# A feature-major prologue with pipelined modulation, and a new order of the S5 tables in a hybrid S5, attention and experts layer

## The chip, the cores and the metric

One core of a Trainium2 chip. The metric is the device time of one launch in microseconds (us); less is better. An execution of this kernel repeats within about 0.3%.

## What is computed

One layer over 512 latent tokens `x` and 256 context tokens `ctx`, 1024 features, all in float32. Only the latent stream leaves the layer. Cut to what matters here:

```python
mod_x = silu(c) @ w_ada + b_ada            # 6 x 1024; mod_c from c_ctx in the same way
hx = rmsnorm(x, g1) * (1 + sc1x) + sh1x    # hc from ctx in the same way
u, qa, kva, kr, gates = split(hx @ w_in)   # 512 | 384 | 256 | 32 | 2048 columns; for hc without the gates
attn = mla(qa, [kv_c, kv_x], [kr_c, kr_x]) @ w_mla_o          # 8 heads, latents see context and latents
lam_bar, b_bar = discretise(lam, log_dt, b)                   # complex, 32 groups x 64 states, 2 directions
y = d * u + sum over directions of Re(c_out @ scan(lam_bar, b_bar @ u))   # state starts from the context's
ssm = (gelu(y) * sigmoid(gelu(y) @ w_glu + b_glu)) @ w_ssm_o
x = x + g1x * ((sigmoid(g_ssm) * ssm + sigmoid(g_attn) * attn) @ w_out)
x = x + g2x * expert_choice(modulated rmsnorm(x))             # 16 SwiGLU experts of width 2816, 64 tokens each
```

## The kernel before

Float32 weights and activations are split into two float32r parts (`hi`, `lo`), and a product is three matmuls (`mm3`, L121 to L124: L122 hi*hi, L123 hi*lo, L124 lo*hi). All up to L983 is one stage whose order on each engine is as written (`tc.manual_schedule()`, L212); the attention, the merge and the experts behind it are ordered by the framework. `dma` issues on SyncE's queue. T, V, S, G in the code are TensorE (PE), VectorE (DVE), ScalarE (ACT) and GpSimd (POOL).

**Prologue.** X (32 context and 64 latent rows of eight tokens each) is loaded token-major in eight DMAs, then `craw`, `braw` and the 16 tiles of the first third of `w_ada`. ACT squares X with a row sum, `xnorm` (L332) makes the reciprocal root mean square and VectorE scales X; `xt_half` (L344) turns X into feature-major tiles `xTa`, `xTb` (latent) and `hc` (context) with 64 PE transposes and their evictions. Between these, VectorE works out the S5 tables (exponentials, powers `lp`, their spreads `lt` and `lq` at L409, rotations `e8`, `bbar` from `bbar_g` at L454). `ada_part` (L189) makes the modulation with 32 output rows for each of four column blocks; `ada_end` (L193) copies it (`adar`), turns it into columns by eight small transposes (`adac`) and adds the bias (`acol`), from which `ab` follows. Then a loop over eight blocks of 128 features (L634 to L644) makes `hi` on ACT, `hxf` and `lo` on VectorE.

**Projection.** `w_in` is taken in 25 blocks of 128 columns (four `u`, two `kv`, three `q`, sixteen `g` for gates) and `kr`. `win_prep` (L609) splits a loaded block (`raw` pool) into `ws` (ACT copy, VectorE subtraction). `win_block` (L651) is 24 matmuls `px`, three for each feature block; `ctx_block` (L659) is 8 x 2 matmuls `pc` for the context. `fill_one` draws the next block after the `u` blocks in the order of L600, as work for PE between the steps of the S5 branch.

**S5 branch**, four groups `gb` of channels. `s5_P` (L508; ten operations on GpSimd, tile `PT`), `s5_Q` (L522; ten on VectorE), `s5_R` (L572; a table of powers by doubling, 24 multiplies and adds on GpSimd, tile `R`), `s5_B` (transposes `pbt` of Q), `s5_K` (L548; matmuls `pkc` of PT, copies `kc` on VectorE, DMAs that lay out `M`), `s5_V` (L756; matmuls `pv`, twelve products `za`, `zb` and sums, two scans at L778, eight operations to `Xc`), `s5_Y` (L790; `py` from M and U, L801 `py` from PT and Xc), `s5_T` and `s5_out`. `PT`, `R` and `ptmp` have two buffers each. Group order: P(0) and R(0) are issued in the prologue, Q(0) ahead of u0, B(0) behind u1, K(0), P(1), R(1) behind u2; in the loop (L842) stand V, two blocks, Q of the next group, Y, U of the next, P and R of the group after the next, a block, T, a block, then K and B of the next group.

**Behind it** attention and merge, with the other two thirds of `w_ada` (`wada_tiles`, L1173, 1 MB a DMA), then the experts, whose weights (2 MB a DMA) go through a ring of ten buffers in the memory that the attention part leaves.

## Time and profile before

| | |
|---|---|
| runs | 1924.98, 1919.36, 1923.01 us, median 1923.01 |
| profiled execution | 1919.85 us, its span 1918.1 us |
| granted TensorE clock, mean | 0.965 |
| PE, busy | 1633.8 us (85%) |
| DVE, busy | 531.5 us (28%) |
| ACT, busy | 320.7 us (17%) |
| POOL, busy | 209.9 us (11%) |
| read from HBM | 623.93 MB |

The experts take from about 650 us to the end; the change lies in the first 270 us. A row of a timeline gives start, duration, engine, line, operation, output and inputs with their shapes, and in brackets the idle time ahead of it and what ended that. A windows row gives busy time and number of instructions for each engine, the granted clock as a share of 2.4 GHz, the DMA share and GB/s.

### The profile page before, as it was taken

The numbers are of one execution on the slowest core, as the hardware profiler recorded it, in microseconds if no ns is written. First come the engines' busy times: TensorE is split into PE (matmuls) and PEld (weight loads), VectorE is DVE, ScalarE is ACT, GpSimd is POOL, SyncE is SP. The second block draws the span as 40 slices with busy tenths as digits, with TensorE's granted clock in tenths as the row PEclk, the third lists the DMA queues.
The fourth block names the chain that finished last, engine by engine and source line by source line (L and its number), as shares of the span: only waits on it lengthen the run. The fifth ranks groups of instructions, "written<-read, shape, count | busy, mean of one in ns | idle before, by whom it ended". The sixth has DMA issues, their size and how long they took to land.

```text
span 1918.1 us, 20921 instructions
## 1 busy us (share of the span) xinstructions
PE 1633.8 (85%) x8660; PEld 791.5 (41%) x8660; DVE 531.5 (28%) x1180; ACT 320.7 (17%) x593; POOL 209.9 (11%) x218
## 2 busy tenths in 40 slices
...
GB/s 316 57 141 111 105 189 133 170 97 201 157 90 401 363 422 426 422 427 420 422 427 422 421 426 422 426 423 423 425 421 427 421 427 421 420 428 421 427 422 281
DMA packets 108654, 642.56 MB, mean 335 GB/s; under 512 B 10256, under 2 KB 45072, under 8 KB 73232
## 3 DMA queue, kind: packets, MB, share of 16 engines
...
q14 instruction: 26, 0.21, 0.0%
HBM read 623.93 MB, written 17.27 MB: 334 GB/s over the span
## 4 chain that ended last, share of the span: by engine, by line
PE 43%; DMA 36%; DVE 8%; issue 5%; ACT 3%; POOL 2%; POOLq 0%; ACTq 0%; SPq 0%; DVEq 0%
DMA wgu<-in_w_e_gu 18%; PE pgu L1505 14%; DMA wd<-in_w_e_down 10%; PE pdn L1520 8%; DMA wd<-in_w_e_down_end 6%; PE pxg L1462 2%; PE po L1263 1%; DVE hd L94 1%; PE px L122 1%; PE px L124 1%; PE px L123 1%; ACT hd L1507 1%; PE ada L191 1%; PE phT L1512 1%; PE py L801 1%
## 5 line engine op out<-in xcount | busy, mean ns | idle before, releaser
L1505 PE MATMUL pgu<-wgu,xe 128*64 128x512 f32 (+1 forms) x3072 | 644.9, 559 | 27.5 <-DMA wgu<-in_w_e_gu 26.0
L1505 PEld LDWEIGHTS pgu<-wgu,xe 128*64 128x64 f32 x3072 | 219.9, 137 | 426.5 <-issue 351.1
L1520 PE MATMUL pdn<-wd,hT 128*64 128x512 f32 x1408 | 357.5, 645 | 34.5 <-ACT hT L1514 34.5
L94 DVE TENSOR_TENSOR hd<-hd,pgu 64x512 f32<-64x512 f32 x96 | 61.9, 645 | 994.3 <-ACT hd L1507 994.3
L1507 ACT ACTIVATE hd<-pgu 64x512 f32<-64x512 f32 x96 | 53.3, 556 | 951.5 <-PE pgu L1505 951.5
L1520 PEld LDWEIGHTS pdn<-wd,hT 128*64 128x64 f32 x1408 | 110.9, 146 | 214.2 <-issue 163.6
L1539 POOL DMA_INDIRECT out<-ye,sidx x16 | 24.9, 1556 | 1340.7 <-DVE ye L112 1340.7
L1512 PE MATMUL phT<-pk,hd 64*128 64x64 f32 x352 | 42.1, 236 | 126.7 <-DVE hd L94 126.7
L1512 PEld LDWEIGHTS phT<-pk,hd 64*128 64x128 f32 x352 | 29.0, 138 | 204.3 <-DVE hd L94 204.3
L122 PE MATMUL px<-hx,ws 128*128 128x512 f32 x200 | 81.1, 406 | 6.3 <-ACT hx L637 6.3
L123 PE MATMUL px<-hx,ws 128*128 128x512 f32 x200 | 80.1, 400 | 3.5 <-DVE hx L94 3.4
L124 PE MATMUL px<-hx,ws 128*128 128x512 f32 x200 | 79.5, 398 | 1.4 <-DVE ws L94 1.4
L1462 PE MATMUL pxg<-xm,oh 128*64 128x512 f32 x256 | 75.3, 609 | 0.6 <-DVE oh L94 0.6
L1514 ACT COPY hT<-phT 128x256 f32<-128x256 f32 x96 | 34.1, 355 | 119.2 <-PE phT L1512 119.2
L122 PEld LDWEIGHTS px<-hx,ws 128*128 128x128 f32 x200 | 38.4, 192 | 15.3 <-ACT hx L637 6.4
L123 PEld LDWEIGHTS px<-hx,ws 128*128 128x128 f32 x200 | 38.1, 190 | 14.7 <-DVE hx L94 7.6
L124 PEld LDWEIGHTS px<-hx,ws 128*128 128x128 f32 x200 | 38.2, 191 | 10.2 <-DVE ws L94 2.5
L1466 DVE COPY xg<-pxg 128x256 f32<-128x256 f32 x16 | 6.8, 424 | 127.1 <-ACT xg L1465 127.1
L1462 PEld LDWEIGHTS pxg<-xm,oh 128*64 128x64 f32 x256 | 30.6, 140 | 21.1 <-issue 19.4
L1233 DVE TENSOR_REDUCE mx<-ps 128x1 f32<-128x768 f32 x32 | 30.5, 954 | 27.7 <-PE ps L124 25.0
L354 PE MATMUL xT<-pk,X 96*128 96x96 f32 x64 | 11.5, 348 | 29.1 <-DMA craw<-in_ssm_c 18.7
L191 PE MATMUL ada<-wada,scv 128*32 128x512 f32 x192 | 34.1, 675 | 0.0
...
## 6 DMA issues: line engine op xcount, KB each, us to landing
wgu<-in_w_e_gu SPq DMA_DIRECT2D x176, 2048.0 KB, 37.9
...
```

Source lines behind the costliest of these rows:

```text
L94: (e or V).tensor_tensor(o, a, b, op=op)
L122: T.matmul(o, a[0], b[0], start=first, stop=False)
L123: T.matmul(o, a[0], b[1], start=False, stop=False)
L124: T.matmul(o, a[1], b[0], start=False, stop=last)
L191: T.matmul(p[32 * q:32 * q + 32, :], scv[:, k].rearrange("p s n -> p (s n)"), w[q], start=(k == 0), stop=(k == 7))
L1233: V.tensor_reduce(mx, p[:, 0:768], AX.X, ALU.max, negate=True)
L1462: T.matmul(px[64 * h:64 * h + 64, :], oh[:, t], xms[t][:, 512 * h:512 * h + 512], start=(t == 0), stop=(t == 3))
L1505: T.matmul(p[64 * j:64 * j + 64, :fn], xe[:, k, :], wt_[8 * j + k], start=(k == 0), stop=(k == 7))
L1507: S.activation(hd[:, :fn], p[0:64, :fn], AF.Silu)
L1512: T.transpose(ph[:, b, :], hd[:, 128 * b:128 * b + 128], ident[0:64, 0:64])
L1514: S.copy(hT[:, :n], ph[:, :n])
L1520: T.matmul(po[64 * h:64 * h + 64, :], hT[:, b, :], w[:, 512 * h:512 * h + 512], start=(f0 == 0 and b == 0), stop=(f0 + 128 * b == FF - 128))
```

## The change

- The host lays out `x` and `ctx` feature-major (`xt`, `ct`) and `w_in`, `w_kr` and `w_ada` by blocks, so that a partition's part of a tile is one run of 2 to 4 KB. The loads write 128 partitions each. The order on SyncE's queue is now: parameters, four `xt` and two `ct` pieces, six `w_ada` tiles of 1 MB, u0, four `w_ada` tiles of 512 KB, u1 to u3, `braw`, `craw`, `wkr`.
- The transposes, their evictions and the scaling of X go. `sums` squares on ACT (12 operations) and adds on VectorE (15 operations in `acc`), six matmuls sum over the features, `rstd` is [128, 6], and six matmuls spread it over the partitions in PSUM (`rb`).
- `lp`'s later powers, the two spreads and `bbar_g` are functions of their own: `powers_lp` and the spread of `lq` stand behind the `ada` matmuls, `bbar_g`, Q(0) and the spread of `lt` behind the first two `u` blocks.
- The modulation loop makes `hxf` one step ahead on VectorE (with `rb`), `hi` on ACT, `lo` on VectorE, and PE does the six matmuls of u0 and u1 for that feature block within the loop, into `px01`.
- P(0) is issued behind Q(0) and `lt`; R(0) on VectorE, R(1) on GpSimd. In the loop K(gb) stands first; P(gb+1) stands behind Y(gb) in place of P(gb+2), and `PT` has one buffer. One gate block more is drawn ahead of the loop. `uf` has two buffers. The three copies of `f_kr` go to ACT. The later `w_ada` tiles come in two DMAs of 512 KB each. The tail has four steps in place of five.

```diff
-                 ("rt", 1), ("rr", 2), ("xc", 1), ("pt", 2), ("m4", 2), ("uu", 1), ("yb", 1)):
+                 ("rt", 1), ("rr", 2), ("xc", 1), ("pt", 1), ("m4", 2), ("uu", 1), ("yb", 1),
+                 ("uf", 2)):
...
-    xv = A["x"].rearrange("(c l) d -> c l d", l=L)
-    cv = A["ctx"].rearrange("(c l) d -> c l d", l=L)
-    X = []
-    for j in range(4):
-        t = tl("xx", f"X{j}", [NCH, 2, D])
-        dma(t[0:NCX], cv[:, 2 * j:2 * j + 2, :])
-        dma(t[NCX:NCH], xv[:, 2 * j:2 * j + 2, :])
-        X.append(t)
+    hc = tl("hxp", "hc", [128, 8, 256])
+    xt = [tl("pt", "xTa", [128, 4, 512]), tl("bt", "xTb", [128, 4, 512])]
+    for i in range(2):
+        for j in range(2):
+            k = 2 * j
+            dma(xt[i][:, k:k + 2, :], A["xt"][i, :, k:k + 2, :])
+        dma(hc[:, 4 * i:4 * i + 4, :], A["ct"][:, 4 * i:4 * i + 4, :])
+    wt = {}
+    def wada_load(kh, tags):
...
+    wada_load(0, ["hxp", "hxp"])
+    wada_load(1, ["hxp", "hxp"])
+    wada_load(2, ["ws", "ws"])
+    order = [(f, b) for f, bs in (("u", range(4)), ("g", (0, 1, 2)), ("kv", (0,)), ("g", (3, 4, 5)), ("kv", (1,)),
+                                  ("g", (6, 7, 8)), ("q", (0, 1)), ("g", (9, 10)), ("q", (2,)), ("g", range(11, 16)))
+             for b in bs]
+    base = {"u": 0, "q": 4, "kv": 7, "g": 9}
+    wins, preps = [], {}
+    nxt = {"load": 0, "prep": 0}
...
+    win_load()
+    wada_load(3, ["m4", "m4", "zz", "xc"])
+    win_load()
+    win_load()
+    win_load()
+    braw = tl("qq", "braw", [128, 2, 32, 16])
+    dma(braw, A["ssm_b"])
     craw = cst("craw", [128, 2, 32, 16], p="early")
     dma(craw, A["ssm_c"])
-    braw = tl("qq", "braw", [128, 2, 32, 16])
-    dma(braw, A["ssm_b"])
-    hc = tl("hxp", "hc", [128, 8, 256])
...
-    wada_load(0, [("hxp", 1), ("hxp", 1)])
-    wada_load(1, [("hxp", 1), ("hxp", 1)])
-    wada_load(2, [("m4", 0), ("m4", 0), ("rr", 0), ("rr", 0)])
+    wkr = tl("kr", "wkr", [128, 8, 32])
+    dma(wkr, A["w_kr"])
...
+    acc = tl("sq", "acc", [128, 768])
+    def sums():
+        for i in range(2):
+            for j in range(4):
+                sq = tl("gt", "sqx", [128, 512]) if i or j else acc[:, 0:512]
+                S.activation(sq, xt[i][:, j, :], AF.Square)
+                if i or j:
+                    add(acc[:, 0:512], acc[:, 0:512], sq)
+                    yield
+            for j in range(0, 4, 2):
+                sq = tl("gt", "sqc", [128, 2, 256])
+                S.activation(sq, hc[:, 4 * i + j:4 * i + j + 2, :], AF.Square)
+                if i or j:
+                    add(sq[:, 0], sq[:, 0], sq[:, 1])
+                    add(acc[:, 512:768], acc[:, 512:768], sq[:, 0])
+                else:
+                    add(acc[:, 512:768], sq[:, 0], sq[:, 1])
...
-    def xnorm(hf):
-        l0 = 4 * hf
-        vx = sm("vx", [NCH, 4])
-        ts(vx, ssx[:, l0:l0 + 4], 1.0 / D, EPS)
-        yield
-        yield from rsqrt_g(rstd[:, l0:l0 + 4], vx, [NCH, 4])
-        for l in range(l0, l0 + 4):
-            ts(X[l // 2][:, l % 2, :], X[l // 2][:, l % 2, :], rstd[:, l:l + 1])
+    rstd = cst("rstd", [128, 6])
+    def xnorm():
+        pss = pa("pssx", (128, 6))
+        for t in range(6):
+            T.matmul(pss[:, t:t + 1], acc[:, 128 * t:128 * t + 128], ones, start=True, stop=True)
+        for _ in range(9):
             yield
-    xt = []
-    def xt_half(hf):
-        if not hf:
-            xt.extend([tl("pt", "xTa", [128, 4, 512]), tl("bt", "xTb", [128, 4, 512])])
-        for kp in range(4):
...
+        ssx = sm("ssx", [128, 6])
+        ts(ssx, pss, 1.0 / D, EPS)
+        yield
+        yield from rsqrt_g(rstd, ssx, [128, 6])
...
-    rr(xnorm(1), late_by(2, powers2()), late_by(2, powers()), late_by(8, xt_half(0)))
-    wada_load(3, [("zz", 0), ("xc", 0), ("xx", 1)])
+    rr(powers2(), late_by(2, powers()))
+    rr(rot(), late_by(3, xnorm()))
     pada = pg("ada0")
-    for k in range(2):
-        ada_part(pada, k, [wt[0, q][:, k] for q in range(4)])
-    rr(xt_half(1), rot(), late_by(8, bbar_g()))
-    for k in range(2, 8):
+    for k in range(4):
         ada_part(pada, k, [wt[k // 2, q][:, k % 2] for q in range(4)])
+    rb = pw("rb")
+    for t in range(6):
+        T.matmul(rb[:, t // 4, 128 * (t % 4):128 * (t % 4) + 128], rstd[:, t:t + 1].to_broadcast([128, 128]), ident,
+                 start=True, stop=True)
+    for k in range(4, 8):
+        ada_part(pada, k, [wt[k // 2, q][:, k % 2] for q in range(4)])
+    rr(powers_lp())
+    for k in (0, 4):
+        c = hc[:, k:k + 4, :]
+        mul(c, c, rb[:, 1, None, 0:256].to_broadcast([128, 4, 256]))
+    rr(spread(lq, 1, 0))
...
-    def s5_R(gb):
+    def s5_R(gb, e=G):
+        mk = dtl if e is V else (lambda nm, sh_: tl("ptmp", nm, sh_))
         cs = slice(8 * gb, 8 * gb + 8)
         R = tl("rr", "R", [128, 2, 8, NCH])
-        G.memset(R[:, 0, :, 0:1], 1.0)
-        G.memset(R[:, 1, :, 0:1], 0.0)
-        G.tensor_copy(R[:, :, :, 1:2], e8[:, 0, :, cs, None])
+        e.memset(R[:, 0, :, 0:1], 1.0)
+        e.memset(R[:, 1, :, 0:1], 0.0)
+        e.tensor_copy(R[:, :, :, 1:2], e8[:, 0, :, cs, None])
         n, j = 2, 1
         while n < NCH:
-            e = min(n, NCH - n)
-            cmul(R[:, :, :, n:n + e], R[:, :, :, 0:e], e8[:, j, :, cs, None].to_broadcast([128, 2, 8, e]), [128, 2, 8, e],
-                 lambda nm, s: tl("ptmp", nm, s), G)
-            n, j = n + e, j + 1
+            m = min(n, NCH - n)
+            cmul(R[:, :, :, n:n + m], R[:, :, :, 0:m], e8[:, j, :, cs, None].to_broadcast([128, 2, 8, m]), [128, 2, 8, m], mk, e)
+            n, j = n + m, j + 1
         RTs[gb] = R
...
-    s5_P(0)
-    s5_R(0)
-    pha.close()
...
-    ada_end(0, pada, tl("dt", "adar0", [128, 512]), win_prep)
+    win_prep()
+    ada_end(0, pada, tl("dt", "adar0", [128, 512]))
     ab1 = cst("ab1", [128, 2, 8, 2])
     c0 = acol[:, 0].rearrange("p (u q) b s -> p u (q b) s", u=2)
     V.tensor_copy(ab1[:, 1], c0[:, 0])
     stt(ab1[:, 0], c0[:, 1], 1.0, P("g1n")[:, :, None].to_broadcast([128, 8, 2]), ALU.add, ALU.mult)
+    win_prep()
     hx = [[tl("hxp", f"hx{i}{j}", [128, 4, 512], F32R) for j in range(2)] for i in range(2)]
-    for k in range(8):
-        x = xt[k // 4][:, k % 4, :]
-        hi, lo = [hx[i][k // 4][:, k % 4, :] for i in range(2)]
-        S.activation(hi, x, AF.Identity, scale=ab1[:, 0, k, 0:1], bias=ab1[:, 1, k, 0:1])
-        S.activation(hc[:, k, :], hc[:, k, :], AF.Identity, scale=ab1[:, 0, k, 1:2], bias=ab1[:, 1, k, 1:2])
-        h = tl("gt", "hxf", [128, 512])
-        ts(h, x, ab1[:, 0, k, 0:1], ab1[:, 1, k, 0:1])
-        sub(lo, h, hi.bitcast(F32))
-        if k == 0:
-            ws, raw = preps["u", 0]
-            sub(ws[:, 1], raw, ws[:, 0].bitcast(F32))
     def hxs(k, tok=slice(0, 512)):
         return [hx[i][k // 4][:, k % 4, tok] for i in range(2)]
+    pf = pw("px01")
+    first = [preps.pop(("u", b)) for b in range(2)]
+    def hc_mod(k):
+        S.activation(hc[:, k, :], hc[:, k, :], AF.Identity, scale=ab1[:, 0, k, 1:2], bias=ab1[:, 1, k, 1:2])
+    def modulated(k):
+        h = tl("gt", "hxf", [128, 512])
+        stt(h, xt[k // 4][:, k % 4, :], ab1[:, 0, k, 0:1], rb[:, 0, :], ALU.mult, ALU.mult)
+        return h
+    h = modulated(0)
+    for k in range(8):
+        hi, lo = hxs(k)
+        S.activation(hi, h, AF.Identity, bias=ab1[:, 1, k, 0:1])
+        hn = modulated(k + 1) if k < 7 else None
+        if k:
+            hc_mod(k - 1)
+        stt(lo, h, ab1[:, 1, k, 0:1], hi.bitcast(F32), ALU.add, ALU.subtract)
+        h = hn
+        for j in range(2):
+            mm3(pf[:, j, :], [first[j][0][:, i, k, :] for i in range(2)], hxs(k), k == 0, k == 7)
+    hc_mod(7)
...
-        V.tensor_copy(kr4[:, 0:512], px)
-        V.tensor_copy(kr4[:, 512:768], pc)
+        S.copy(kr4[:, 0:512], px)
+        S.copy(kr4[:, 512:768], pc)
         pk_ = pa("pkrt", (128, 6, 32))
         for t in range(6):
             T.matmul(pk_[:, t, :], kr4[:, 128 * t:128 * t + 128], P("stack"), start=True, stop=True)
-        V.tensor_copy(krt, pk_)
+        S.copy(krt, pk_)
...
+    win_prep()
+    us_ = {}
+    for b in range(2):
+        pc = ctx_block(first[b][1])
+        win_load()
+        u_out(b, pf[:, b, :], pc)
+        if b == 0:
+            us_[0] = s5_U(0)
+    rr(bbar_g())
     s5_Q(0)
-    o = f_u(0)
-    win_prep()
-    u_out(0, *o)
-    us_ = {0: s5_U(0)}
-    o = f_u(1)
-    win_prep()
-    u_out(1, *o)
-    s5_B(0)
+    rr(spread(lt_, 0, 1))
+    s5_P(0)
     o = f_u(2)
-    s5_bd(0)
     win_prep()
     u_out(2, *o)
-    s5_K(0)
-    s5_P(1)
+    s5_R(0, V)
     s5_R(1)
     o = f_u(3)
     win_prep()
     u_out(3, *o)
+    s5_bd(0)
+    s5_B(0)
+    fill_one()
+    win_prep()
     for gb in range(4):
         U, rt = us_.pop(gb)
+        s5_K(gb)
+        if gb < 3:
+            s5_bd(gb + 1)
         Xc = s5_V(gb, U, rt)
         fill_one()
         fill_one()
@@ -871,9 +896,8 @@
         yb = s5_Y(gb, U, Xc)
         if gb < 3:
             us_[gb + 1] = s5_U(gb + 1)
-            s5_bd(gb + 1)
+            s5_P(gb + 1)
         if gb < 2:
-            s5_P(gb + 2)
             s5_R(gb + 2)
         fill_one()
         t, y = s5_T(gb, yb)
@@ -884,7 +908,6 @@
             f_kr()
         fill_one()
         if gb < 3:
-            s5_K(gb + 1)
             s5_B(gb + 1)
             win_prep()
...
-            dma(wt[g][q], wada_src(1 + g // 2, 4, g % 2, q))
+            for kh in range(2):
+                dma(wt[g][q][:, kh], wada_src(1 + g // 2, 2 * (g % 2) + kh, q, 1))
```

VectorE from the end of the prologue to the first modulated tile; `acol` and `ab` are the modulation as columns, `hxf` a modulated tile, `ws` a split weight block. Before:

```order
L107 TENSOR_SCALAR e_219<-nw 128x32
L94 TENSOR_TENSOR acol<-adac_693,pk 128x32
L631 COPY ab_699<-acol 128x16
L112 SCALAR_TENSOR_TENSOR ab_699<-acol,pk 128x16
L109 TENSOR_SCALAR hxf<-xTa,ab_699 128x512
L94 TENSOR_TENSOR hx_704<-hxf,hx_702 128x512
L94 TENSOR_TENSOR ws<-win_u_679,ws 128x1024
L109 TENSOR_SCALAR hxf<-xTa,ab_699 128x512
```

Now:

```order
L94 TENSOR_TENSOR ws<-win_u_176,ws 128x1024
L94 TENSOR_TENSOR acol<-adac_507,pk 128x32
L633 COPY ab_513<-acol 128x16
L112 SCALAR_TENSOR_TENSOR ab_513<-acol,pk 128x16
L94 TENSOR_TENSOR ws<-win_u_186,ws 128x1024
L112 SCALAR_TENSOR_TENSOR hxf<-xTa,ab_513,rb 128x512 x2
L112 SCALAR_TENSOR_TENSOR hx_521<-hxf,ab_513,hx_519 128x512
L112 SCALAR_TENSOR_TENSOR hxf<-xTa,ab_513,rb 128x512
```

The first `ws` subtraction has moved ahead of `acol`, a second one stands between `ab` and the first `hxf`, and `hxf` is made a step ahead.

R(0): before, on GpSimd, behind P(0) in the prologue:

```order
L94 TENSOR_TENSOR PT<-PT,pu 128x512
L575 MEMSET R 128x8
L576 MEMSET R 128x8
L577 COPY R<-e_219 128x16
L94 TENSOR_TENSOR cm_u<-R,e_219 128x32
L94 TENSOR_TENSOR cm_w<-R,e_219 128x32
L94 TENSOR_TENSOR R<-cm_u,cm_w 128x8x2 x2
```

Now on VectorE, behind the spread of `lt` and the split of the first gate block (of its doublings the first and the last are shown, with what stands behind):

```order
L428 COPY lt<-lp 128x2x32 x8
L107 TENSOR_SCALAR lt<-lt 128x256
L94 TENSOR_TENSOR ws<-win_g_627,ws 128x1024
L603 MEMSET R 128x8
L604 MEMSET R 128x8
L605 COPY R<-e_221 128x16
L94 TENSOR_TENSOR cm_u<-R,e_221 128x32
...
L94 TENSOR_TENSOR R<-cm_u,cm_w 128x8x32 x2
L94 TENSOR_TENSOR ws<-win_g_655,ws 128x1024
L94 TENSOR_TENSOR ws<-win_g_762,ws 128x1024
L584 COPY kc<-pkc_960 128x112
```

`R(0)` has moved from GpSimd to VectorE, and the splits of the second and third gate block and the copies of K(0) stand behind it.

PE around K of group 1 (`px` a projection block, `pkc` K, `pbt` B, `pv` V). Before:

```order
L123 MATMUL px<-hx_705,ws 128x512
L124 MATMUL px<-hx_703,ws 128x512
L554 MATMUL pkc_1447<-PT,bd 32x128 x16
L539 MATMUL pbt<-pk,Q 128x128 x16
L767 MATMUL pv<-U,BT 64x96 x32
```

Now:

```order
L123 MATMUL px<-hx_522,ws 128x512
L124 MATMUL px<-hx_520,ws 128x512
L566 MATMUL pbt<-pk,Q 128x128 x16
L581 MATMUL pkc_1398<-PT,bd 32x128 x16
L784 MATMUL pv<-U,BT 64x96 x32
```

K has moved behind B, next to V.

## Rows read from the trace of the kernel before

**Rows 1.** Windows: stretch, length, busy (count) of PE, PEld, DVE, ACT, POOL, clock, DMA share, GB/s

```profile
250.00:300.00 50.00, 49.17 (x305) 39.39 (x304) 30.66 (x66) 16.91 (x21) 1.34 (x2) 1.00 0.55 184
650.00:1900.00 1250.00, 1061.47 (x5204) 388.98 (x5202) 111.13 (x303) 90.42 (x201) 23.35 (x15) 0.97 1.01 423
```

**Rows 2.** Chain that ended last, in order of time: the last wait of each group's Y

```profile
123.36 0.87 PE py L801 x12
...
169.00 1.55 PE py L801 x12
...
220.53 0.87 PE py L801 x12
...
260.48 0.87 PE py L801 x12
```

**Rows 3.** Timeline, prologue: the parameters, the end of the modulation, block u0's first and last matmul

```profile
4.08 0.21 ACT L242 ACTIVATE sc2v<-pk 128x8 f32<-128x8 f32 x1 [2.05 <-DMA pk<-in_pk]
...
51.70 1.06 PE L199 MATMUL adac<-pk,adar 128*128 128x8 f32 x8 [0.71 <-ACT adar L194]
...
57.64 0.18 DVE L94 TENSOR_TENSOR acol<-adac,pk 128x32 f32<-128x32 f32 x1
...
59.09 0.80 PE L122 MATMUL px<-hx,ws 128*128 128x512 f32 x1 [6.34 <-ACT hx L637]
...
74.30 0.40 PE L124 MATMUL px<-hx,ws 128*128 128x512 f32 x1
```

**Rows 4.** Windows, two stretches of the first loads (X, then w_ada)

```profile
12.00:14.00 2.00, 0.00 (x0) 0.00 (x0) 0.00 (x0) 1.47 (x3) 0.00 (x0) 1.00 0.98 217
22.00:24.00 2.00, 0.99 (x7) 0.69 (x5) 1.94 (x19) 0.92 (x2) 0.00 (x0) 1.00 1.05 408
```

**Rows 5.** Line 191 up to 60 us: ns min/median/max, first and last start

```profile
L191 PE MATMUL ada<-wada,scv x64: 592/780/1062, 29.3 to 50.4; 128*32 128x512 f32 x64
```

**Rows 6.** Timeline, VectorE and GpSimd beside each other and apart

```profile
79.69 2.07 POOL L94 TENSOR_TENSOR PT<-craw,lt 128x1024 f32<-128x1024 f32 x1
79.89 2.42 DVE L94 TENSOR_TENSOR qu<-bbar,lq 128x512 f32<-128x512 f32 x1
...
95.39 1.27 POOL L94 TENSOR_TENSOR PT<-PT,pu 128x512 f32<-128x512 f32 x1
...
177.60 2.00 POOL L94 TENSOR_TENSOR PT<-craw,lt 128x1024 f32<-128x1024 f32 x1
...
190.56 1.28 POOL L94 TENSOR_TENSOR PT<-PT,pu 128x512 f32<-128x512 f32 x1
...
223.00 1.22 DVE L94 TENSOR_TENSOR Q<-bbar,lq 128x1024 f32<-128x1024 f32 x1
224.14 0.68 DVE L94 TENSOR_TENSOR qu<-bbar,lq 128x512 f32<-128x512 f32 x1
```

**Rows 7.** Timeline, a multiply of 256 on VectorE and one of 32 on GpSimd

```profile
24.40 0.42 DVE L94 TENSOR_TENSOR cm_u<-lp 128x256 f32<-128x256 f32 x1
...
193.07 0.25 POOL L94 TENSOR_TENSOR cm_u<-R,e 128x32 f32<-128x32 f32 x1
```

**Rows 8.** Windows, a stretch of the modulation loop with block u0

```profile
60.00:70.00 10.00, 6.35 (x12) 3.28 (x12) 9.60 (x10) 8.86 (x15) 7.59 (x7) 0.50 0.00 0
```

**Rows 9.** Timeline, PE: block u2's first matmul and its context part

```profile
89.19 0.48 PE L122 MATMUL px<-hx,ws 128*128 128x512 f32 x1
...
94.75 3.61 PE L662 MATMUL pc<-hc,win_u 128*128 128x256 f32 x16
```

**Rows 10.** Timeline, VectorE: the first product of V(0)

```profile
110.09 0.56 DVE L94 TENSOR_TENSOR za__1091<-pv,R 128x384 f32<-128x384 f32 x1 [2.26 <-PE pv L767]
```

**Rows 11.** Timeline, PE: the end of Y(0), then K(1) and V(1)

```profile
127.31 1.09 PE L801 MATMUL py<-PT,Xc 64*64 64x128 f32 x16
...
145.71 1.08 PE L554 MATMUL pkc<-PT,bd 128*32 128x128 f32 x32
...
149.64 2.86 PE L767 MATMUL pv<-U,BT 128*64 128x96 f32 x64
```

More of the change, by code (lines that the diff above doesn't have):

```diff
@@ L202, in ada_end, with wada_src @@
         rows[t] = r
-    def wada_src(t, kn, kh, q):
-        return wada[:, kn * kh:kn * kh + kn, (4 * t + q) * 512:(4 * t + q + 1) * 512]
-    pha = ph1.enter_context(ExitStack())
-    for n, k in (("xx", 4), ("jk", 1)):
-        cur[n] = pool(n, pha, bufs=k)
+    def wada_src(t, kh, q0, qn):
+        return A["w_ada"][t, kh, :, q0:q0 + qn]
+    for n, k in (("sq", 3), ("gt", 3), ("kr", 1), ("ws", 2), ("raw", 4)):
+        cur[n] = pool(n, ph1, bufs=k)
     man = ph1.enter_context(ExitStack())
@@ new lines, in hybrid_block @@
+    wt = {}
+    def wada_load(kh, tags):
+        n = len(tags)
+        for i, tag in enumerate(tags):
+            t = tl(tag, f"wada{kh}{i}", [128, 4 // n, 2, 512])
+            dma(t, wada_src(0, kh, 4 // n * i, 4 // n))
+            for j in range(4 // n):
+                wt[kh, 4 // n * i + j] = t[:, j]
+    wada_load(0, ["hxp", "hxp"])
[4 more added lines that the diff above has]
+             for b in bs]
@@ new lines, in hybrid_block, with win_load @@
+    base = {"u": 0, "q": 4, "kv": 7, "g": 9}
+    wins, preps = [], {}
+    nxt = {"load": 0, "prep": 0}
+    def win_load():
+        if nxt["load"] < len(order):
+            f, b = order[nxt["load"]]
+            nxt["load"] += 1
+            w = tl("raw", f"win_{f}{b}", [128, 8, 128])
+            dma(w, A["w_in"][base[f] + b])
+            wins.append(w)
+    win_load()
[4 more added lines that the diff above has]
+    braw = tl("qq", "braw", [128, 2, 32, 16])
@@ L294, in expm1_parts @@
         yield
-    ssx = cst("ssx", [NCH, L])
-    rstd = cst("rstd1", [NCH, L])
-    for l in range(L):
-        jk = tl("jk", "sqj", [NCH, D])
-        S.activation(jk, X[l // 2][:, l % 2, :], AF.Square, accum_out=ssx[:, l:l + 1])
+    acc = tl("sq", "acc", [128, 768])
[16 more added lines that the diff above has]
+                yield
     dtv, za, zb = c32("dtv"), c32("za"), c32("zb")
```

91 lines of the change are left out of this document (27 added, 64 removed).

## The prediction

> **What bounds the kernel now.** Read the windows of the whole program first. From 650 to 1900 us the experts' weights set the pace: the DMA share is 1.01 at 423 GB/s [rows 1]. What comes before is one serial stretch on TensorE: between 250 and 300 us PE is busy 49.17 of 50 us while the DMA share is 0.55 [rows 1]. The expert weights go into memory that the attention part frees, so what is won or lost ahead of that part moves the end by as much; I carry it over one to one. Then the chain of waits: in that stretch it hangs on the first group's `Y` at 123.36 us, and the later groups' `Y` follow after 45.6, 51.5 and 40.0 us [rows 2]. So the question is by how much `Y(0)` moves, counted with the PE work that is done by then, and whether the three steps behind it change.
>
> **The load and the way to the first projection matmul.** The parameters are there at about 4 us [rows 3]. X comes at 217 GB/s with a DMA share of 0.98, `w_ada` at 408 [rows 4]. In the change x and ctx (3.15 MB) come into 128 partitions, then 8.39 MB of `w_ada` and one `u` block of 0.52 MB. If all goes at 408 GB/s the last `w_ada` tile is there at 4 + 12.06/0.408 = 33.6 us; if x and ctx still go at 217, at 4 + 3.15/0.217 + 8.91/0.408 = 40.3. I take 33.6: the new loads have the shape of those at 408 (128 partitions, runs of 4 KB), and X has 32 and 64 partitions.
> The Trainium skill ("SBUF — State Buffer", section "Door 1: The DMA port swizzle") says that a transfer into partitions 0 to 31 or 0 to 63 reaches only 8 of 16 ports, at 189 to 196 GB/s. The 217 beside 408 agrees; by it the load ends at 33.6, without it at 40.3.
>
> Behind the last tile stand eight `ada` matmuls, four at a time, 2 x 0.78 = 1.6 us [rows 5], the copy and the eight small transposes (0.71 + 1.06, row of `adac`), and `acol` to the first `px` (59.09 − 57.64 = 1.45) [rows 3]. New in between on VectorE: a `ws` subtraction of 1024 elements (1.22) and the first modulated tile (0.68), by the 1024 and 512 rows when nothing runs beside them [rows 6]. Sum 6.7, so the first `px` starts at **40** us, not 59.09. The 64 transposes, their evictions, the X·rstd scaling and the first group's spread and `bbar` leave this stretch. What VectorE keeps is some 150 instructions ahead of `acol` (117 of 32 elements at 0.18 or less, 9 of 256 at 0.42, 7 of 512 at 0.68, 3 of 1024 at 1.22 [rows 3, 6, 7]): at most 33 us from 4 us on. That just fits under the load: if it misses, 0 to 1 us are lost.
>
> **The first two blocks.** Before, `u0` alone took 59.09 to 74.70 [rows 3], with PE at a granted clock of 0.50 (the 1.2 GHz level) and 12 matmuls in 10 us [rows 8], since each of the eight steps waits for ACT and VectorE. Now 48 matmuls stand in one run, six to each step. A block of 24 takes 89.19 to 94.75 = 5.5 us [rows 9], 0.23 a matmul; at the lower level I count twice that. All at the upper level: 11 us; all at the lower: 22. VectorE needs two operations of 0.68 for a step and PE at least 1.4, so PE isn't starved as before; I take a fifth at the lower level, **13** us. So `u0` and `u1` are done at T = 53. Before, `u0` at 74.7 plus 5.5 for `u1` makes 80.2. **Gain here 27.**
>
> **What the first group gives back.** VectorE's work for group 0 now comes behind T: two `ws` subtractions (2.4), `bbar_g` (12 small ones at 0.18, four 512s, four 256s: 6.6), `Q(0)` (two 1024s, eight 512s: 7.9), `lt` (nine at about 0.2) [rows 3, 6, 7]. So `lt` is ready at T + 19. Only then may GpSimd begin `P(0)`, and VectorE, after the next `ws`, `R(0)`. Both read two operands from SBUF. The rows of before show what that does: `qu` takes 2.42 beside a `PT` of 2.07 that started 0.2 earlier, and 0.68 alone; `P` takes 79.69 to 96.66 = 17.0 beside VectorE's `Q`, 14.2 alone [rows 6]. They take turns, about one operation each. `P(0)` has ten operations, so it ends at T + 36, and `R(0)` has got through about twelve of its 24 multiplies and adds. The twelve left are the large ones: 4 of 512, 6 of 256, 2 of 128, 5.7 us alone; between them GpSimd now does `R(1)`'s small ones (0.25 each [rows 7]), some 4 us more. `R(0)` ends at T + 46. In order behind it on VectorE stand two `ws` subtractions (the second gate waits for one) and the five copies of `K(0)`, so the `za` row starts at T + 50. From `za` to the last wait of `Y(0)` it was 110.09 to 123.36 = 13.3 [rows 2, 10]; with `R(1)` beside the SBUF-only ones at the end I take 15.5. `Y(0)` at 53 + 50 + 15.5 = **118.5**. PE meanwhile has `pc` (3.6 each) and two `u` blocks, `B`, one gate: some 33 us from T, and it waits. One gate more than before is done by then, so the old mark is 123.36 + 5.5 = 128.9. **Gain left: 10.**
> The Trainium skill (same page, section "Who interferes with whom") says that VectorE and GpSimd share a port pair by an exclusive lock, held for a whole instruction, when VectorE has two SBUF inputs. The 2.42 against 0.68 agrees. By it `R(0)` on VectorE beside `P(0)` is no parallel work; without it the sum is the first rival's.
>
> **The later steps.** The same matmuls stand in them. Now `K(gb+1)` waits for `P(gb+1)`, which, with one PT buffer, can't start before `Y(gb)` has read the old one. Before, PE had 128.4 to 145.71 = 17.3 us between `Y(0)` and `K(1)` [rows 11], and `B` (149.64 − 145.71 − 1.08 = 2.9) now comes ahead: 20.2 us for `P(1)`. Group 1 has `f_kr` as well, so more; group 2 has a `q` block without the `pc` (3.6): 16.6. Against `P` at 14.2 to 17.0, 19 at most where V's neighbours run: nothing, nothing, and 1 to 3 us in the last step. The one gate drawn ahead and `kr`'s three copies now on ACT give about as much back in the first two. **Sum 0.** The modulation tiles' 32 DMAs in place of 16 lie beside PE work at a share of 0.55 [rows 1]: nothing.
>
> **Sum.** 1919.85 us is the profiled execution (span 1918.1); minus 10 is 1910. The median of the runs is 1923.0, 3.2 above the profiled one, so on the runs' scale 1923.0 − 10 = **1913**. For the forecast alone: 1907 to 1918 (VectorE late by 1, `V` 13.3 or 17, the clock's 11 or 15).
>
> **Rivals.**
> 1. *The two engines don't hinder each other here.* `R(0)` then ends with `P(0)`, which takes 14.2 to 17: `Y(0)` at T + 53 = 106, a gain of 23 and **1900**. For it: the trace shows few such pairs, and `R`'s operands are laid out otherwise than `Q`'s. Against: the `qu` row. Chance 0.20.
> 2. *x and ctx load as slowly as X.* t = 40.3, and all behind it moves by 6.7: **1920**, no change that can be measured. Against: 408 GB/s for 128 partitions. Chance 0.13.
> 3. *Slower: `P` becomes the bound of every group.* The place is `K(gb+1)` on PE behind `P(gb+1)`. If each of the ten operations alternates with one of VectorE's (`P` = 25: 17.0 plus eight more turns of about 1), PE waits 25 − 20.2 = 4.8, then 0, then 25 − 16.6 = 8.4, and for the lower level after each pause I add 3 [rows 8]: 16 lost, 10 won: **1929**. It decides from about 23 us for `P`. For it: VectorE runs `V`, `Q` and `ws` there without a pause. Against: 17.0 beside `Q`. Chance 0.07.
> 4. *The pipelined modulation stays at the lower level*: 22 us in place of 13, **1922**. For it: 0.50 in that place before [rows 8]. Against: there PE waited in each step. Chance 0.08.
>
> **How the numbers follow.** The forecast has 0.52. A measurement here tells 0.3% (5.8 us) from no change. Faster: the forecast without its upper end and rival 1, 0.73; slower: rival 3 and a little, 0.08; the rest 0.19. The range 1900 to 1923 leaves out rival 3 and what lies under rival 1.
>
> **What would show it.** Right: last `w_ada` tile near 34 us, first `px` near 40, the 48 matmuls over by 53 with a rising clock; VectorE's large `R` multiplies at 1 to 2 us beside `PT` rows; PE waiting at `K(0)` and the gate behind it for VectorE; `Y(0)` near 118; its steps 44 to 52 as before. Wrong: `R` multiplies at 0.68 beside `PT` (rival 1), 217 GB/s up to 14 us (rival 2), waits before `pkc` on GpSimd of several us (rival 3), 0.45 a matmul through `px01` (rival 4).

## The result, and the profile after

The changed kernel takes 1904.59 us (median of 1903.6 to 1905.41, four runs), beside 1921.37 us before: ratio 0.991, 95% interval 0.9893 to 0.9928, so it is faster by 0.9%, 17 us. The forecast was 10 us. Its profiled execution took 1903.6 us, span 1901.8. Run once more in a later batch, the changed kernel had a median of 1906.71, and three of its six executions (1907.6 to 1912.5 us) show a granted clock of 0.946 to 0.948 where the others show 0.965 to 0.969; so differences of a few microseconds between two kernels are read from the traces below and not from medians.

The end of the prologue on PE in the profile after (timeline: start, duration, engine, line, operation, in brackets the idle time ahead and what ended it); it answers to [rows 3]:

```profile
34.85 1.90 PE L190 MATMUL ada<-wada,scv 128*32 128x512 f32 x10 [0.23 <-DMA wada<-in_w_ada]
37.43 1.06 PE L198 MATMUL adac<-pk,adar 128*128 128x8 f32 x8 [0.68 <-ACT adar L193]
41.61 0.80 PE L122 MATMUL px<-hx,ws 128*128 128x512 f32 x1 [3.12 <-ACT hx L656]
...
47.25 0.45 PE L122 MATMUL px<-hx,ws 128*128 128x512 f32 x1
47.54 0.39 PE L123 MATMUL px<-hx,ws 128*128 128x512 f32 x1
...
55.48 4.69 PE L679 MATMUL pc<-hc,win_u 128*128 128x256 f32 x21
```

The last wait for `w_ada` ends at 34.85, the first projection matmul starts at 41.61 in place of 59.09, and the 48 matmuls of u0 and u1 are through at T = 55.48. The first twelve take 5.6 us (0.47 each), at a granted clock of 0.50 (the 1.2 GHz level, windows from 42 to 47 us); the rest take 0.23 each, at 1.00 from 47.5 us on.

The chain that ended last, in order of time, after; it answers to [rows 2]:

```profile
113.81 1.54 PE py L818 x12
...
160.19 1.54 PE py L818 x12
...
210.13 0.87 PE py L818 x12
...
250.12 0.87 PE py L818 x12
```

`Y(0)` waits until 113.81 in place of 123.36. The steps behind it are 46.4, 49.9 and 40.0 us; before they were 45.6, 51.5 and 40.0. `Y(3)` is 260.48 − 250.12 = 10.4 us earlier, with one gate block (5.5) more behind it done: 15.9 us. The spans differ by 16.3. So nearly all was won ahead of `Y(0)` (0.8 us in the steps behind it), and it went to the end one to one: the first matmul of the attention (`pkt`) starts at 307.3 in place of 323.1.

Between T and `Y(0)` two engines decide, after. First VectorE's timeline: small operations of R(0), some of its large ones with the last, the first product of V(0):

```profile
77.59 0.19 DVE L94 TENSOR_TENSOR cm_u<-R,e 128x32 f32<-128x32 f32 x1
77.70 1.26 DVE L94 TENSOR_TENSOR cm_w<-R,e 128x32 f32<-128x32 f32 x1
...
80.08 1.28 DVE L94 TENSOR_TENSOR cm_u<-R,e 128x64 f32<-128x64 f32 x1
81.28 1.96 DVE L94 TENSOR_TENSOR cm_w<-R,e 128x64 f32<-128x64 f32 x1
...
88.24 0.42 DVE L94 TENSOR_TENSOR cm_u<-R,e 128x256 f32<-128x256 f32 x1
...
92.47 0.89 DVE L94 TENSOR_TENSOR cm_w<-R,e 128x512 f32<-128x512 f32 x1
93.40 0.97 DVE L94 TENSOR_TENSOR R<-cm_u,cm_w 128x256 f32<-128x256 f32 x2
...
98.16 0.55 DVE L94 TENSOR_TENSOR za__1014<-pv,R 128x384 f32<-128x384 f32 x1
```

Then GpSimd's timeline: `P(0)`'s first and last operation with two from its middle, and one operation of `R(1)` and the same one of `R(2)`:

```profile
73.21 2.11 POOL L94 TENSOR_TENSOR PT<-craw,lt 128x1024 f32<-128x1024 f32 x1 [12.53 <-DVE lt L428]
...
80.01 1.27 POOL L94 TENSOR_TENSOR PT<-PT,pu 128x512 f32<-128x512 f32 x1
81.24 1.92 POOL L94 TENSOR_TENSOR PT<-craw,lt 128x1024 f32<-128x1024 f32 x1
...
86.70 1.29 POOL L94 TENSOR_TENSOR PT<-PT,pu 128x512 f32<-128x512 f32 x1
...
89.76 0.73 POOL L94 TENSOR_TENSOR cm_u<-R,e 128x64 f32<-128x64 f32 x1
...
139.15 0.30 POOL L94 TENSOR_TENSOR cm_u<-R,e 128x64 f32<-128x64 f32 x1
```

Up to 88 us the small multiplies of `R(0)`, all but the first, take 1.1 to 2.0 us beside `P(0)`, where 0.2 to 0.3 is their own time: the twelve small multiplies and adds take 77.59 to 88.24 = 10.7 us. The rows show why: a multiply of VectorE ends just behind the operation of GpSimd that it stands beside, the one of 1.28 us at 81.36 behind 81.28, the one of 1.96 us at 83.24 behind 83.16. From 88.24 on, beside the small operations of `R(1)`, the large ones take little more than they take alone (0.42 for 0.42, 0.89 for 0.68), and it is GpSimd that pays: 0.73 for an operation that takes 0.30 with nothing beside it. `P(0)` took 73.21 to 87.99 = 14.8.

### The profile page after: what moved, and what is told of

It is laid out like the page before. It is cut to its first block, busy times and chain, and to the rows that moved or that the text cites. A ratio compares the mean times of both kernels' runs of the same rounds, so it can differ in the third digit from the quotient of the medians.

```text
span 1901.8 us, 20811 instructions
## 1 busy us (share of the span) xinstructions
PE 1631.7 (86%) x8620; PEld 791.5 (42%) x8620; DVE 531.6 (28%) x1192; ACT 314.9 (17%) x584; POOL 192.7 (10%) x191
## 4 chain that ended last, share of the span: by engine, by line
PE 42%; DMA 39%; DVE 9%; issue 6%; ACT 3%; POOL 0%; POOLq 0%; ACTq 0%; SPq 0%; DVEq 0%
DMA wgu<-in_w_e_gu 20%; PE pgu L1533 13%; DMA wd<-in_w_e_down 11%; PE pdn L1548 8%; DMA wd<-in_w_e_down_end 6%; PE pxg L1490 2%; PE po L1291 2%; DMA wada<-in_w_ada 1%; PE px L122 1%; DVE hd L94 1%; PE px L124 1%; PE px L123 1%; ACT hd L1535 1%; PE ada L190 1%; PE py L818 1%
## 5 line engine op out<-in xcount | busy, mean ns | idle before, releaser
L1261 DVE TENSOR_REDUCE mx<-ps 128x1 f32<-128x768 f32 x32 | 30.5, 954 | 24.7 <-PE ps L124 22.7
L1264 ACT ACTIVATE pr<-ps,mx 128x768 f32<-128x768 f32 x32 | 28.9, 903 | 10.8 <-DVE mx L1261 5.9
```

## The experiments

The question: is the stretch from T to `V(0)` set by turns that the two engines take (theory A), or do they work side by side, so that `P(0)` alone or something else sets it (theory B)? Times of the kernels are medians, with the ratio to before and its interval, which reaches some 3 to 7 us to either side; the changed kernel is the 1904.59 above (1906.71 when run again). Between two of these kernels a total alone therefore shows no difference of 2 or 3 us; the start of `za` and the last wait of `Y(0)` do.

**R(0) back on GpSimd.**

```diff
-    s5_R(0, V)
+    s5_R(0)
```

> One part of the change undone: R(0) back on GpSimd behind P(0). Theory A (VectorE's operations with two SBUF inputs and GpSimd's take turns, so only the sum of both counts): in the changed kernel R(0) took 17.7 us beside P(0) and R(1), and P(0) 14.7. Here P(0) runs from 73.2 to 87.5 as before, R(0) then takes 14.4 (R(3) by itself on GpSimd in the trace of before: 191.8 to 206.2), so R(0) is there at 102, the first za at 102 instead of 98.2, Y(0) some 3 us later, total +3 to +4 us against the changed kernel (1907 to 1909). Theory B (the two engines work side by side, R(0) on VectorE is free): R(0) on VectorE saved the whole 14.4, so this costs 10 us or more (1915).

Measured 1908.74 us (ratio to before 0.9942, 0.9923 to 0.996). `R(0)` ran from 88.8 to 103.5, the first `za` came at 102.80, 4.6 us later than in the changed kernel, and `Y(0)` at 121.42, since `R(1)` then lay beside all of `V(0)` (18.6 us in place of 15.65). `za` and the total, 4 us more, are as A said; B's 10 us or more are out. `Y(0)` was 7.6 us later, where A had 3; 3 us of that came back behind it. Moving `R(0)` to VectorE was worth 4 us, not the 14 us that it takes on GpSimd.

**R(0) ahead of P(0).**

```diff
+    s5_R(0, V)
     rr(spread(lt_, 0, 1))
     s5_P(0)
...
-    s5_R(0, V)
```

> R(0) stays on VectorE, but ahead of the spread of lt and so ahead of P(0), with nothing beside it. Theory A: R(0) takes 8 us instead of 17.7, lt and P(0) start 8 us later (81 us), P(0) ends at 95.5 with little beside it, K(0) and pv follow on PE to 99.5, za at 98 to 99.5: the total within 2 us of the changed kernel (1904.6), since the two together cost the same in either order. Theory B: P(0) simply starts and ends 8 us later, R(0) had not been in its way: K(0), V(0) and the total 6 to 8 us later (1911).

VectorE's timeline in this kernel, `R(0)`'s first operation, one of its small multiplies, the first of its last twelve operations, and what follows its last:

```profile
71.67 0.17 DVE L605 COPY R<-e 128x16 f32<-128x16 f32 x1
...
72.65 0.22 DVE L94 TENSOR_TENSOR cm_w<-R,e 128x64 f32<-128x64 f32 x1
...
74.15 0.42 DVE L94 TENSOR_TENSOR cm_u<-R,e 128x256 f32<-128x256 f32 x1
...
79.47 0.61 DVE L428 COPY lt<-lp 128x64 f32<-128x64 f32 x4
```

PE's timeline in this kernel:

```profile
94.49 1.08 PE L581 MATMUL pkc<-PT,bd 128*32 128x128 f32 x16 [5.10 <-POOL PT L94]
```

With nothing beside it `R(0)` takes 71.67 to 79.47 = 7.8 us, not the 17.8 (76.56 to 94.37) of the changed kernel; the multiply that took 1.96 there takes 0.22, and the last twelve operations take 5.4 where they took 6.1. `K(0)` now waits 5.1 us for `P(0)`, which started 7 us later. `za` starts at 100.30, `Y(0)` at 117.52, the total is 1907.08 (0.9932, 0.9914 to 0.995), 2.5 us more than the changed kernel. `za` is 2.1 us later and `Y(0)` 3.7: nearer to A (within 2) than to B (6 to 8), but A's `za` at 98 to 99.5 was missed too. The 10 us saved on `R(0)` all came back as a later `P(0)`.

**lt and P(0) first.**

```diff
     hc_mod(7)
+    rr(spread(lt_, 0, 1))
...
+    s5_P(0)
     win_prep()
     win_prep()
...
-    rr(spread(lt_, 0, 1))
-    s5_P(0)
```

> The spread of lt and P(0) moved from behind Q(0) to right behind the modulation loop, where VectorE idles from 51.1 to 56.1 and GpSimd has nothing; R(1) follows P(0) at once. Theory A: P(0) runs 52.7 to 68 and R(1) from 68 on, beside bbar, Q(0) and R(0) on VectorE, whose operations each wait for one of GpSimd's; the 5 us idle are used but R(1)'s 14 us come into the same stretch: za between 95 and 108, V(0) afterwards 2 us shorter, total from -4 to +6 us (1900 to 1911). Theory B: P(0) and R(0) are out of each other's way, VectorE's list ends near 84, za starts when pv is through at 93: total 5 to 8 us less (1897 to 1899).

Measured 1902.56 us (0.99, 0.988 to 0.9919). `P(0)` ran from 52.77 to 68.4, as meant, and `R(1)` from there to 90. `za` started at 100.09, 2 us later than in the changed kernel though `P(0)` was done 20 us earlier: theory B's 93 is out. `V(0)` behind it ran as an undisturbed one does. PE's last wait in `Y(0)` is another one here:

```profile
112.32 0.69 PE L813 MATMUL py<-M,U 128*64 128x128 f32 x4 [3.44 <-DMA gs<-gt]
```

The row names the store of a gate; of these matmuls' own operands `M` comes by DMAs that are issued behind `K(0)`'s copies, up to 109.6, so which of the two ended the wait is open. The matmuls that mark `Y(0)` in the other kernels follow without a wait, at 113.43, 0.4 us earlier than in the changed kernel.

**R(0) on GpSimd in the prologue.**

```diff
     rr(rot(), late_by(3, xnorm()))
+    s5_R(0)
     pada = pg("ada0")
...
-    s5_R(0, V)
```

> R(0) on GpSimd as early as its inputs are there (behind rot, about 30 us), beside the load of w_ada and the ada matmuls, so nothing of it is left behind the first two blocks. Theory A: VectorE's own prologue, which idled 2.3 us before acol, is slowed by some 2 to 4 us, so the first px is at 42 to 44 instead of 41.6; behind it R(0)'s 17.7 us are gone from VectorE, P(0) runs alone to 87.5, K(0) at 88, za at 90 to 92 instead of 98.2: total 4 to 7 us less (1898 to 1901). Theory B: R(0) was hidden by P(0) anyway, nothing gained behind, 0 to 3 us lost in the prologue: 1904 to 1908.

Measured 1909.92 us (0.9944, 0.9925 to 0.9964): 5 us more than the changed kernel, and both expectations missed. VectorE's timeline in the prologue of this kernel (an operation of `powers_lp`, and `acol`):

```profile
35.00 1.29 DVE L94 TENSOR_TENSOR cm_u<-lp 128x256 f32<-128x256 f32 x1
...
43.31 0.19 DVE L94 TENSOR_TENSOR acol<-adac,pk 128x32 f32<-128x32 f32 x1
```

The same two in the changed kernel:

```profile
30.49 0.42 DVE L94 TENSOR_TENSOR cm_u<-lp 128x256 f32<-128x256 f32 x1
...
38.53 0.19 DVE L94 TENSOR_TENSOR acol<-adac,pk 128x32 f32<-128x32 f32 x1 [2.30 <-PE adac L198]
```

The twelve operations of `powers_lp` took 29.70 to 38.87 = 9.2 us beside `R(0)`'s large ones, where they took 28.84 to 31.69 = 2.9. A had priced that with 2 to 4 us of VectorE's time and the first `px` at 42 to 44. VectorE lost 6.3 us there and 0.9 ahead of it, of which only 2.3 were idle before, so the first `px` came at 46.39, 4.8 later. From there to `za` it was 51.1 in place of 56.6, a gain of 5.4 where A had some 8.6, and `V(0)`, now with `R(1)` beside all of it, took 2 us more. `Y(0)` came at 115.14, 1.3 us later than in the changed kernel.

**lt and P(0) first, R(0) on GpSimd.** The edit of the third experiment, and `s5_R(0)` in place of `s5_R(0, V)`.

> As tables_first (lt and P(0) right behind the modulation loop), but with R(0) on GpSimd behind P(0), so that R(0) leaves VectorE's list and R(1) comes after it. Theory A (turns): GpSimd has P(0) and R(0), 29 us alone, from 52.8 on, VectorE some 20 us of its own in the same stretch; in tables_first 59 us of work of both took the 47 us from 52 to 99 us, so these 49 take about 39: R(0) is there at 90 to 92, za at 91 to 93 instead of 100.1 there and 98.2 in the changed kernel, V(0) 15 to 17 us beside R(1): total 4 to 7 us less than the changed kernel (1898 to 1901), 2 to 4 less than tables_first. Theory B (no turns): R(0) ends at 82, za when pv is through at 91 to 93: the same total; the two differ in GpSimd's end of R(0), 90 against 82, and in VectorE's end of Q(0), later than 78 by turns against 73.

Measured 1900.09 us (0.9895, 0.9861 to 0.9929): the total that both theories gave. What tells them apart is inside: `R(0)` was through at 90.3 (A: 90 to 92; B: 82) and `Q(0)` at 83.5 (A: later than 78). `za` came at 95.27, later than expected, since the split of the third gate stands ahead of it and waited 6.2 us for ACT's copy; `Y(0)` at 112.25.

**u0 and u1 one after the other.**

```diff
-        for j in range(2):
-            mm3(pf[:, j, :], ..., hxs(k), k == 0, k == 7)
+        mm3(pf[:, 0, :], ..., hxs(k), k == 0, k == 7)
+    for k in range(8):
+        mm3(pf[:, 1, :], ..., hxs(k), k == 0, k == 7)
```

> The pipelining taken apart: the modulation loop keeps the 24 matmuls of u0 only, and those of u1 come behind the loop. Theory A (six matmuls a step keep PE busy, so that its clock rises and u1 is hidden behind the modulation): the loop is then paced by VectorE's 1.33 us a step, u0 ends at 52.5, u1 takes 5.5 to 10 more: the two are done at 58 to 62 instead of 55.5, and the total is 3 to 6 us more than the changed kernel (1907 to 1911). Rival: PE would have done the 48 in the same time in any order, since VectorE's pace sets the end: 55 to 56, total within 1 us.

Measured 1903.46 us (0.9917, 0.9889 to 0.9945): not to be told from the changed kernel. Its 48 matmuls were through at 57.44, 2 us later, and `Y(0)` at 115.39, 1.6 later. A missed, and the end of the 48 lies between A's 58 to 62 and the rival's 55 to 56; the total is the rival's, within 1.1 us. PE waits in three of the later steps (0.34 to 0.36 us, for `lo`), but its clock rose all the same (granted clock 0.50 up to 46 us, 1.00 from 46.5 on), and u1 ran at 0.23. So six matmuls a step are worth 2 us at T, and nothing that the total shows. Of the rest of the 24.7 us up to T, 17.5 are the earlier first `px`; the other 5 go with what this kernel keeps (the lookahead of `hxf` among it), and no run takes these apart.

**x and ctx in halves of 64 partitions.**

```diff
-            dma(xt[i][:, k:k + 2, :], A["xt"][i, :, k:k + 2, :])
+            for h in (slice(0, 64), slice(64, 128)):
+                dma(xt[i][h, k:k + 2, :], A["xt"][i, h, k:k + 2, :])
```

(and the same for `ct`)

> Each xt and ct piece loaded as two transfers, partitions 0 to 63 and 64 to 127, in place of one into 128. If a transfer into 64 partitions is served at the 217 GB/s that X had, whatever stands behind it in the queues, the load of 3.15 MB takes 14.5 us instead of some 7.5, the last w_ada tile is 7 us later (41 instead of 34.7) and the total 6 to 7 us more (1911). If the two halves run beside each other, the 12 to 14 us window shows 400 GB/s or more and the total is the same within 1 us.

Windows of the first loads in this kernel (columns as in [rows 1]):

```profile
8.00:10.00 2.00, 0.00 (x0) 0.00 (x0) 1.76 (x10) 0.96 (x3) 0.00 (x0) 1.00 1.03 234
...
12.00:14.00 2.00, 0.00 (x0) 0.00 (x0) 1.66 (x8) 0.97 (x3) 0.00 (x0) 1.00 1.06 244
```

The same stretches in the changed kernel:

```profile
8.00:10.00 2.00, 0.00 (x0) 0.00 (x0) 1.90 (x9) 1.37 (x3) 0.00 (x0) 1.00 1.02 342
...
12.00:14.00 2.00, 0.00 (x0) 0.00 (x0) 1.97 (x10) 1.39 (x3) 0.00 (x0) 1.00 1.05 440
```

The same bytes with runs of the same length go at 234 to 244 GB/s in halves and at 342 to 440 whole, although the second half stands right behind the first in the queue. The DMA share is 1.03 to 1.06 in the halves, so the DMA engines did not idle between the transfers. A half is also a smaller transfer, 256 KB in place of 512; what that alone costs, no run here shows. The last `w_ada` wait ends at 39.59 in place of 34.85, `Y(0)` is at 117.63, 3.8 us later, and the total is 1907.51 us (0.9926, 0.9902 to 0.9951), 3 us more. The direction is the first expectation's; its 41 and 1911 were too much.

**The small operations of bbar first**, with the changed kernel beside it.

```diff
     hc_mod(7)
+    bb = bbar_g()
+    for _ in range(9):
+        next(bb)
+    rr(spread(lt_, 0, 1))
...
-    rr(bbar_g())
+    rr(bb)
```

(on top of the kernel with `P(0)` first and `R(0)` on GpSimd)

> tables_first_g with bbar's twelve small operations ahead of lt, so that they stand in VectorE's idle stretch behind the modulation loop and not beside P(0). Theory A': a turn costs an engine the length of the other's operation that is under way, so VectorE's small operations pay most beside GpSimd's long ones (there the twelve took 59.85 to 68.29 = 8.4 us, 2.4 alone) and GpSimd pays most beside VectorE's long ones. The twelve then take 2.4 to 2.6; lt and P(0) start 2.4 us later (54.5); P(0) beside ws and bbar's and Q's large operations takes 16 to 17.5 instead of 15.7; Q(0) ends at 79 to 81 instead of 83.5, K(0) at 88 to 89 instead of 91.3, za at 92 to 93.5 instead of 95.3: total 2 to 3 us less than tables_first_g, 5 to 7 less than the changed kernel (1897 to 1899). Rival: a turn costs a fixed microsecond whatever the lengths; then the large operations pay the same 8 us beside P(0), Q(0) ends where it did and the total stays within 1 us of tables_first_g (1900).

> The changed kernel itself, beside the next two on one chip: 1903 to 1906 by either theory, Y(0)'s last wait at 113 to 114.

Measured 1900.87 us (0.9903, 0.9889 to 0.9918) beside 1906.71 (0.9941, 0.9927 to 0.9955) for the changed kernel. The twelve small operations take 51.86 to 54.23 = 2.4 us, as said. But the eight of `bbar` that now stand beside `P(0)` take 60.38 to 72.80 = 12.4 us, where they take 60.79 to 64.79 = 4.0 in the changed kernel. So a turn costs VectorE what is left of GpSimd's operation, whatever VectorE's own length is, here about 1 us for each of the eight, and the total stays that of the kernel without this edit, as the rival said. The rival's fixed microsecond would give the same 8 us; the rows of the changed kernel, 1.28 us beside an operation of 1.27 and 1.96 beside one of 1.92, speak for GpSimd's length. GpSimd pays too, by VectorE's operations: `P(0)` takes 55.13 to 72.58 = 17.4 beside these large ones, 15.7 beside the small ones, 14.8 beside `R(0)`'s in the changed kernel.

**R(1) only behind V(0).**

```diff
-    ... ("rr", 2), ("xc", 1), ...
+    ... ("rr", 1), ("rq", 1), ("xc", 1), ...
-        R = tl("rr", "R", [128, 2, 8, NCH])
+        R = tl("rq" if gb == 2 else "rr", "R", [128, 2, 8, NCH])
```

> small_first with one buffer shared by R(0), R(1) and R(3) and one for R(2), so that R(1) can't start before V(0) has read R(0). Theory A': nothing of GpSimd stands beside V(0), which then takes 13.3 to 14 us from za to Y(0)'s last wait instead of 17; R(1) runs from 107 to 123 beside ws and Q(1), P(1) behind it until 139 to 141, where K(1) needs it at about 138: Y(0) 3 us earlier than small_first, up to 3 of it lost again at K(1) and by Q(1): total 0 to 3 us less than small_first (1895 to 1898). Rival: V(0) takes 17 us for its own reasons (the scans): no gain, and P(1) late: 2 to 4 us more than small_first.

PE's timeline in this kernel:

```profile
106.73 0.87 PE L822 MATMUL py<-PT,Xc 64*64 64x128 f32 x12 [1.56 <-DVE Xc L94]
...
132.45 0.43 PE L581 MATMUL pkc<-PT,bd 128*32 128x128 f32 x8 [1.14 <-POOL PT L94]
139.89 1.08 PE L581 MATMUL pkc<-PT,bd 128*32 128x128 f32 x16 [7.01 <-POOL PT L94]
142.24 0.66 PE L581 MATMUL pkc<-PT,bd 128*32 128x128 f32 x8 [1.27 <-POOL PT L94]
```

With nothing of GpSimd beside it `V(0)`, from `za` on, takes 93.53 to 106.73 = 13.2 us (94.02 to 112.36 = 18.3 in the kernel with the small operations first), and `Y(0)` is at 106.73, 7 us earlier than in the changed kernel. Then `K(1)` waits 9.4 us for `P(1)`, which stands behind `R(1)` on GpSimd, and `Y(1)` is at 163.06, 2.9 us later than in the changed kernel: 1908.02 us (0.994, 0.9922 to 0.9959). This is the prediction's third rival, brought about by an order that the change doesn't have.

**R(0) on VectorE behind two splits.** The kernel with the small operations first, with `s5_R(0, V)` behind the split that follows u3, and `s5_R(1)` right behind `P(0)`.

> small_first with R(0) on VectorE again, but behind the splits of the first two gates, where VectorE idles 7.7 us in small_first, and R(1) on GpSimd right behind P(0). Theory A' (a turn costs the length of the other engine's operation): R(1) is over by 90 to 92 and no longer stands beside V(0), which takes 13.2 us from za to Y(0)'s last wait as in r1_after_v0 (18.3 in small_first); R(0) starts at 83 beside the second half of R(1), ends at 92 to 94, za at 95 to 97 instead of 94.0: Y(0) at 108 to 110 instead of 112.4, P(1) is not behind anything: total 2 to 4 us less than small_first (1897 to 1899). Rival: with K(1) and the later groups as the bound the earlier Y(0) is given back: within 1 us of small_first.

> small_first once more, for the comparison on one chip: 1900 to 1902 by either theory, Y(0)'s last wait at 112 to 113.

Measured 1901.85 us (0.9903, 0.9878 to 0.9927) beside 1900.67 (0.989, 0.987 to 0.991): no difference, as the rival said of the total, but not for its reason. `V(0)` took 13.2 us, as expected, but `R(0)` took 82.67 to 97.2 beside the large operations of `R(1)`, so `za` came at 99.21 and `Y(0)` at 112.41.

Five orders (the changed kernel, the two with `P(0)` first, the two with the small operations first) put `Y(0)` at 113.8, 113.4, 112.3, 112.4 and 112.4, and the one that takes 14 us of GpSimd's work out of the stretch put it at 106.7. The other orders put it later: 115.1 with `R(0)` in the prologue, where the first `px` was 4.8 us later, 117.5 with `R(0)` ahead of `P(0)`, where GpSimd started 7 us later, and 121.4 with `R(0)` behind `P(0)` on GpSimd, where VectorE idled 10.9 and 9.8 us. So the order does count where it leaves one engine without work. That the five agree because the sum of the work is the same is not shown: `R(0)` takes 7.8 us on VectorE and 14.4 on GpSimd, and in two of the five VectorE idles 6.2 and 7.7 us for a split. What is shown is the turns themselves, in the rows.

## Why the prediction was wrong in its size

- **The load.** 33.6 was forecast, 34.85 measured; from 10 us on it went at 408 to 440 GB/s, before that at 307 to 369, which is the 1 us (estimate: 6 us at some 340 in place of 408). Rival 2 (40.3) did not come about; loading into 64 partitions does bring about what it feared, 39.59. X before was no clean case of that: its latent pieces lay in partitions 32 to 95, only those of the context in 0 to 31. The Trainium skill ("SBUF — State Buffer", section "Door 1: The DMA port swizzle") gives 196 GB/s for a 1 MiB transfer into partitions 0 to 63 and 328 for one into all 128; here it was 234 to 244 in halves and 342 to 440 whole, above the page's figures, but the halves are the slower ones, as the page has it.
- **The first px** at 41.6, not 40: 1.2 us of it is the load. VectorE was in time; it waited 2.30 us for `adac`.
- **The first two blocks.** 13.9 us, not 13; T at 55.5, not 53. Gain 24.7 in place of 27. The clock was at the lower level for twelve matmuls of 48, a quarter (a fifth was taken). Rival 4 did not come about.
- **What the first group gives back: the step that failed.** It was said that `P(0)` would take 17 us and end at T + 36, and that `R(1)`'s small operations would cost VectorE some 4 us, with `R(0)` ending at T + 46. Measured: `lt` at T + 17.7, `P(0)` 14.8 us, to T + 32.5, `R(0)`'s last twelve operations 88.24 to 94.37 = 6.1 where 5.7 had been counted for them alone; end at T + 38.9. Of the 7.1 us, 1.3 lie in `lt`, 2.2 in `P(0)` and 3.6 in the tail. `za` came at T + 42.7 in place of T + 50, `V(0)` took 15.65 (forecast 15.5). T being 2.5 late, `Y(0)` came 4.7 us earlier than forecast.
- The reason: the mechanism held (`R(0)` took 17.8 us beside GpSimd, 7.8 alone, and twelve of its 24 operations were through with `P(0)`, as said), but its price was carried over from another pair: the 17.0 of a `P` that stood beside operations of `Q` and two splits, and the 0.25 us that a small operation of GpSimd lasts. The price goes by the length of the other engine's operation. Those of `Q` and the splits are 0.7 to 1.2 us long; `R(0)`'s first twelve are 0.2 to 0.3, so `P(0)` took 14.8 and not 17.0 (17.4 beside the large ones of `bbar`). And `R(1)`'s first operations held VectorE up by 0.7 us over twelve of its own (6.1 against 5.4 alone), not by the 4 us counted; why VectorE pays so little there, and GpSimd nearly all, no run shows.
- The 14.2 us read as a `P` alone were not quite alone. VectorE's timeline of before has two operations of `Q` beside its start:

```profile
177.73 2.42 DVE L94 TENSOR_TENSOR qu<-bbar,lq 128x512 f32<-128x512 f32 x1
...
180.19 1.43 DVE L94 TENSOR_TENSOR Q<-Q,qu 128x512 f32<-128x512 f32 x1
```

- The Trainium skill (same page, section "Who interferes with whom") has the exclusive lock held for a whole instruction. The rows of `R(0)` beside `P(0)` agree with it, its multiplies ending 0.05 to 0.15 us behind GpSimd's operations, and so do the 7.8 against 17.8 us; the 0.7 us over twelve operations in the tail are less than a turn of 0.25 us for each would cost. Rival 1, no hindrance, is out: it had `Y(0)` at 106.
- **The later steps** summed to 0.8 us of gain (0 forecast). No `K` waited for `P` in this trace (0.9 us for `K(3)` when the kernel was run again), so rival 3 did not come about in this order. Its own sum adds 3 us after each of two pauses but counts them once: 19 lost in place of 16, and 1932.
- **The sum.** 10 forecast, 16.3 in the profiled spans: 128.9 − 113.8 = 15.1 at `Y(0)`, 0.8 in the steps; 0.4 is not assigned.
